# Writing the transposes of the last query tile and of the context's queries later in a hybrid attention kernel

## The chip, the cores and the metric

The kernel runs on one core of one Trainium2 chip. The metric is the device time of one execution in microseconds (us). Before the change it is 1639.22 us, the median of three runs (1639.19 to 1640.38).

## What is computed

Two layers of a trunk are applied to 512 latent tokens and 128 context tokens that share all weights. Each layer is

```
h     = rmsnorm(x) * (1 + scale) + shift
parts = h @ w_in                       # 8 parts
mixed = [ gated linear recurrence | grouped-query attention | differential attention ]
x     = x + gate1 * (mixed @ w_out)
h     = rmsnorm(x) * (1 + scale') + shift'
x     = x + gate2 * (conv_ffn(h))
```

The queries of the grouped attention (8 heads of 64) are normalised per head. Those of the latent tokens are also rotated; those of the context tokens are not. Context tokens attend to context tokens only: 4 groups of 4 score blocks of 128x128 (two groups for the grouped, two for the differential attention). Latent tokens attend to cached context keys and to all latent keys. All is fp32; matrix products split each operand into a rounded part and a rest and add three products.

## The kernel before, in words

The order of the instructions on each engine is written by hand through a small planner. `Flow` keeps a model clock, `fl.now`. Code that emits TensorE products moves the clock on (`fl.step(1296)` after six products, 816 after six narrower ones), and each step first emits the follow-up work whose time has come. `fl.add(delay, fn)` puts work on that list. So a delay does not make the chip wait: it decides behind which products a step is *written*, and each engine then executes its own instructions in the written order. Semaphores, which the tile framework adds, make an instruction wait for its operands and for the buffer it writes.

The part that matters is `mixer`, up to the attention proper. In order:

- Three groups of products (`proj_group`), each four weight chunks by five token tiles by six products of 512 columns: first the queries (`evac_gq` takes the results), then keys, values and differential queries (`evac_kvdq`), then differential keys and values (`evac_dkdv`). The five sums of a group stay in PSUM for the whole group.
- Two narrower sums `lacc` for the recurrence's gate, each in two halves of 24 products of 320 columns; ScalarE reads each half with a Gelu (`lru_in`, L704).
- Then `wait("a")` steps the model clock until 17 pieces of work are written (8 query stacks, 5 key stacks, 4 context groups), and the attention begins with its first scores (L1150).

Between these products TensorE also transposes. For a latent query tile `t` the chain is `s1` (norm), `s2` (rotation), `s2b` (rounded part, GpSimd), `s3` (rest, VectorE, L858), `s4`: four transposes to a tile `qT` (L867) and two ScalarE copies out (L869), once per half of the heads. For the context's queries it is `c2` (VectorE, L878), `c3`: four transposes to `cqT` (L884) and a copy. Key tiles go the same way: `k_stack`, three transposes to `kT` (L905), copies L906 and L910. A key stack needs one of two staging slots ("st"), which query stacks also use.

The context's attention runs beside all this: `ctx_stage` writes four score products (`cS`, L1039), VectorE maxima (`cnm`, L1041) and four ScalarE exponentials (L1044); `ctx_norm` scales the result on VectorE (L1061 to L1068); `ctx_T` transposes it (`cPTp`, L1076) and copies it out (L1078).

PSUM is `pb`: eight single-bank tiles in this part (`psum_mode(0, 8)`). A new tile takes a bank whose last reader has been written, and its first matmul waits until that reader is done. A group's five sums leave three banks for all transposes and context scores; a `cS` of the first two groups takes two of them.

Of the kernel before, what the change touches and what calls it, by code (L numbers as in the profile page):

```python
# [48 lines left out]
GQ = (5150, 3150, 2200, 1400)  # L49


def f32(ap):
    return ap.bitcast(F32)
# [179 lines left out]
def hybrid_kernel(ctx: ExitStack, tc: tile.TileContext, i, o):  # L233
# [13 lines left out]
    fl = Flow()  # L247
    fl.free["st"] = 2

    def half(name, dt=F32):  # L250
        return hpool.tile([128, 2 * W], dt, tag="h", name=name)
# [4 lines left out]
    def tslot(name, n=644, dt=F32):  # L256
        return tp.tile([128, 644], dt, tag="t", name=name)[:, :n]
# [15 lines left out]
    def pb(name, dt=F32):  # L273
        return mode["pb"].tile([128, 512], dt, tag="pb", name=name)
# [5 lines left out]
    def small(name, n=8):  # L280
        return smp.tile([128, 8], F32, tag="sm", name=name)[:, :n]
# [86 lines left out]
    def round_pool(out, in_):  # L368
        pool.tensor_scalar(out=out, in0=in_, scalar1=1.0, scalar2=0.0, op0=ALU.mult, op1=ALU.add)
# [278 lines left out]
    def mixer(l, hh, hl, first=None):  # L648
# [15 lines left out]
        kr, pending = [], {"t": 0.0, "lru": 2, "a": 17}  # L664
# [140 lines left out]
        def rope(src, t, tab, nh, hd):  # L805

            cs, sn = tab[0][:, t], tab[1][:, t]
            e = hd // 4
            tmp = tslot("ropet", nh * hd)
            s5 = src.rearrange("p (h a f e) -> p h a f e", a=2, f=2, e=e)  # L810
            t5 = tmp.rearrange("p (h a f e) -> p h a f e", a=2, f=2, e=e)
            n4 = sn.rearrange("p (a f e) -> p a f e", a=2, f=2)
            for f in range(2):
                dve.tensor_tensor(out=t5[:, :, :, f], in0=s5[:, :, :, 1 - f],
                                  in1=n4[:, :, f].unsqueeze(1).to_broadcast([128, nh, 2, e]), op=ALU.mult)
            s3 = src.rearrange("p (h d) -> p h d", d=hd)
            dve.tensor_tensor(out=s3, in0=s3, in1=cs.unsqueeze(1).to_broadcast([128, nh, hd]), op=ALU.mult)
            dve.tensor_tensor(out=src, in0=src, in1=tmp, op=ALU.add)

        def head_rstd(src, nh):  # L820
            junk = tslot("hsq", nh * 64)
            act.activation(out=junk, in_=src, func=ACTF.Square)
            ss = small("hss", nh)
            dve.tensor_reduce(out=ss, in_=junk.rearrange("p (h d) -> p h d", d=64), op=ALU.add, axis=AX.X)
            return pow_rstd(ss, nh, 1.0 / 64)

        def scale_heads(src, r, nh):
            s3 = src.rearrange("p (h d) -> p h d", d=64)
            dve.tensor_tensor(out=s3, in0=s3, in1=r.unsqueeze(2).to_broadcast([128, nh, 64]), op=ALU.mult)

        def evac_gq(t, a):
            n = tslot("gqr", 512)
            act.activation(out=n, in_=a, func=ACTF.Copy)
            n3 = n.rearrange("p (h d) -> p h d", d=64)
            got = {}

            def s1():
                got["r"] = head_rstd(n, 8)
                if t < 4:
                    fl.add(GQ[1], s2, 2700)  # L840
                else:
                    fl.add(3500, c2, 1300)

            def s2():
                scale_heads(n, got["r"], 8)
                rope(n, t, rope_t["q"], 8, 64)
                for g in range(2):
                    fl.add(100, lambda g=g: s2b(g), 0, "st")

            def s2b(g):  # L850
                st = tslot("gqs", 512, F32R).rearrange("p (h s d) -> p h s d", h=4, s=2)
                hs = slice(4 * g, 4 * g + 4)
                round_pool(st[:, :, g], n3[:, hs])
                fl.add(GQ[2], lambda: s3(g, st), 350)

            def s3(g, st):
                hs = slice(4 * g, 4 * g + 4)
                dve.tensor_tensor(out=st[:, :, 1 - g], in0=n3[:, hs], in1=f32(st[:, :, g]), op=ALU.subtract)  # L858
                fl.add(GQ[3], lambda: s4(g, st))

            def s4(g, st):
                if not qa:
                    for p in range(4):
                        qa[p] = half("qa", F32R)[:, 0:1024].rearrange("p (h c) -> p h c", h=2)
                pt = pb("qT", F32R)
                for h in range(4):
                    pe.transpose(pt[:, h * 128:h * 128 + 128], st[:, h].rearrange("p s d -> p (s d)"), identr)  # L867
                for p in range(2):
                    act.activation(out=qa[2 * g + p][:, :, t * 128:t * 128 + 128],  # L869
                                   in_=f32(pt[:, p * 256:p * 256 + 256].rearrange("p (h c) -> p h c", h=2)),  # L870
                                   func=ACTF.Copy)
                fl.free["st"] += 1
                pending["a"] -= 1
                fl.now += 230

            def c2():
                scale_heads(n, got["r"], 8)
                dve.tensor_tensor(out=n3, in0=n3, in1=rope_t["qg"].unsqueeze(1).to_broadcast([128, 8, 64]), op=ALU.mult)  # L878
                fl.add(2500, c3)

            def c3():
                pt = pb("cqT")
                for b in range(4):
                    pe.transpose(pt[:, b * 128:b * 128 + 128], n[:, b * 128:b * 128 + 128], ident)  # L884
                act.activation(out=cqT, in_=pt[:, 0:512].rearrange("p (b c) -> p b c", b=4), func=ACTF.Copy)
                fl.now += 430

            fl.add(GQ[0], s1, 600)
# [141 lines left out]
        def ctx_probs(qT, kT, kd):  # L1030

            P = tslot("cP", 512).rearrange("p (n c) -> p n c", n=4)
            nm, den, rd = small("cnm", 4), small("cden", 4), small("crd", 4)
# [9 lines left out]
            for n in range(4):  # L1043
                act.activation(out=P[:, n], in_=blkof(n), func=ACTF.Exp, bias=nm[:, n:n + 1], accum_out=den[:, n:n + 1])  # L1044
            return P, den, rd

# [12 lines left out]
        def ctx_norm(n):  # L1059
            P, den, rd = ctxP[n]  # L1060
            dve.reciprocal(out=rd, in_=den)  # L1061
            if n >= 2:
                for j in range(2):
                    dve.tensor_tensor(out=rd[:, 2 * j + 1:2 * j + 2], in0=rd[:, 2 * j + 1:2 * j + 2], in1=neglam[:, l:l + 1],
                                      op=ALU.mult)
            dve.tensor_tensor(out=P, in0=P, in1=rd.unsqueeze(2).to_broadcast([128, 4, 128]), op=ALU.mult)
            if n >= 2:
                dve.tensor_tensor(out=P[:, 0::2], in0=P[:, 0::2], in1=P[:, 1::2], op=ALU.add)  # L1068
            fl.add(CX[3], lambda: ctx_T(n))

        def ctx_T(n):
            P = ctxP[n][0]
            m = 4 if n < 2 else 2
            pt = pb("cPTp")
            for e in range(m):
                pe.transpose(pt[:, e * 128:e * 128 + 128], P[:, e if n < 2 else 2 * e], ident)  # L1076
            dst = cPTg[:, 4 * n:4 * n + 4] if n < 2 else cPTd[n - 2]
            act.activation(out=dst, in_=pt[:, 0:m * 128].rearrange("p (n c) -> p n c", n=m), func=ACTF.Copy)  # L1078
            fl.now += 430
            pending["a"] -= 1  # L1080
# [570 lines left out]
```

## Time and profile before

| | |
|---|---|
| runs | 1639.19, 1639.22, 1640.38 us |
| the profiled execution | 1639.05 us, span 1637.2 us |
| TensorE busy | 1589.8 us, 97% of the span |
| VectorE, ScalarE, GpSimd busy | 58%, 44%, 21% |
| mean granted clock of TensorE | 0.997 of 2.4 GHz |

The profile is of one execution. TensorE works nearly all the time, so an instruction that only moves to another place among its products costs nothing by itself; what matters is where TensorE stands still. A row of the timeline gives the start, the time until the last of the merged instructions ends, and in brackets the idle time just before and what ended it. The modelled end of a matmul lies beyond the start of the next one, so pitches are read from start to start.

### The profile page before, as it was taken

Reading aid. Unit: us, or ns where it says so; the run is one execution under the profiler, and the core shown is the slowest. Engines: PE = TensorE matmul, PEld = TensorE weight load, DVE = VectorE, ACT = ScalarE, POOL = GpSimd, SP = SyncE. Lnnn points to the kernel's source line nnn. Section 1 sums busy time; section 2 is a strip of 40 time slices with the busy share of each in tenths; the row PEclk is TensorE's granted clock in tenths of the full one; section 3 lists DMA queues with packets and bytes.
Section 4 is the critical chain, followed back from the end, with each engine's and each line's share of the span. In section 5 each row is a group of like instructions: output and inputs, shape, how many; then the busy total and the mean of one; then the engine's idle time right before and its main releaser. Section 6 shows DMA issues by size and latency. Waiting matters only on the chain. (4 is left out here: it accounts for less than half of the span.)

```text
span 1637.2 us, 25371 instructions
## 1 busy us (share of the span) xinstructions
PE 1589.8 (97%) x10070; PEld 1396.7 (85%) x10070; DVE 943.5 (58%) x1548; ACT 722.7 (44%) x1476; POOL 351.2 (21%) x782
## 2 busy tenths in 40 slices
PE   6999999999999999999999999999999999999998
PEld 4778776789999889999887787878899998899986
DVE  5687786465555434555467778765555553355544
ACT  4745777544333212333247367774433331133331
POOL 5162443032111000111052614420411100011101
PEclk9999999999999999999999999999999999999999
DMA  9222456412213221222312214352112232121312
GB/s 332 68 87 87 156 192 215 154 52 65 91 52 110 97 77 52 78 78 82 98 33 66 88 60 154 137 187 78 53 52 89 67 129 78 52 78 55 101 65 90
DMA packets 99434, 161.03 MB, mean 98 GB/s; under 512 B 10670, under 2 KB 69222, under 8 KB 94196
## 3 DMA queue, kind: packets, MB, share of 16 engines
q1 hardware_dynamic: 98068, 158.00, 28.9%
q8 instruction: 79, 1.29, 0.3%
q0 software_dynamic: 1040, 1.14, 0.2%
q14 instruction: 39, 0.32, 0.1%
q10 hardware_dynamic: 208, 0.28, 0.0%
HBM read 155.95 MB, written 3.44 MB: 97 GB/s over the span
## 5 line engine op out<-in xcount | busy, mean ns | idle before, releaser
L350 DVE TENSOR_TENSOR wl<-raw,wh 128x1024 fp32r<-128x1024 f32 x180 | 219.9, 1228 | 408.5 <-ACT wh L349 407.5
L365 PE MATMUL uacc<-hl,wh 128*128 128x320 f32 (+2 forms) x1408 | 437.3, 311 | 0.8 <-DVE hl L594 0.5
L364 PE MATMUL uacc<-hh,wh 128*128 128x320 f32 (+2 forms) x1408 | 437.4, 311 | 0.0
L366 PE MATMUL uacc<-hh,wl 128*128 128x320 f32 (+2 forms) x1408 | 435.1, 309 | 0.1
L349 ACT ACTIVATE wh<-raw 128x1024 fp32r<-128x1024 f32 x180 | 189.5, 1058 | 178.9 <-PE tacc L366 156.7
L365 PEld LDWEIGHTS uacc<-hl,wh 128*128 128x128 f32 x1408 | 265.2, 188 | 1.7 <-DVE hl L594 1.6
L366 PEld LDWEIGHTS uacc<-hh,wl 128*128 128x128 f32 x1408 | 265.9, 189 | 0.6 <-DVE wl L350 0.6
L364 PEld LDWEIGHTS uacc<-hh,wh 128*128 128x128 f32 x1408 | 265.5, 189 | 0.3
L364 PE MATMUL tacc<-wh,g 128*128 128x512 f32 x440 | 173.6, 395 | 0.0
L365 PE MATMUL tacc<-wl,g 128*128 128x512 f32 x440 | 173.6, 394 | 0.0
L366 PE MATMUL tacc<-wh,g 128*128 128x512 f32 x440 | 173.1, 393 | 0.0
L1369 POOL TENSOR_SCALAR ca<-u,fcol 128x642 f32<-128x642 f32 x44 | 38.9, 884 | 417.1 <-issue 244.4
L1161 DVE TENSOR_REDUCE nm<-S 128x1 f32<-128x640 f32 x128 | 101.7, 819 | 21.8 <-PE S L1151 11.4
L1176 POOL TENSOR_SCALAR P<-P,den 128x640 f32<-128x640 f32 x96 | 82.5, 865 | 143.4 <-DVE den L1170 77.2
L1165 ACT ACTIVATE P<-S,nm 128x640 f32<-128x640 f32 x128 | 100.8, 792 | 24.9 <-DVE nm L1161 21.4
L1365 ACT ACTIVATE u<-uacc 128x192 f32<-128x192 f32 (+1 forms) x88 | 29.0, 330 | 185.6 <-PE uacc L366 185.6
L366 PEld LDWEIGHTS tacc<-wh,g 128*128 128x128 f32 x440 | 82.7, 188 | 19.4
L364 PEld LDWEIGHTS tacc<-wh,g 128*128 128x128 f32 x440 | 82.6, 188 | 19.3
L365 PEld LDWEIGHTS tacc<-wl,g 128*128 128x128 f32 x440 | 82.7, 188 | 18.9
L364 PE MATMUL acc<-wh,hh 128*128 128x512 f32 x240 | 97.0, 404 | 0.0
L366 PE MATMUL acc<-wh,hl 128*128 128x512 f32 x240 | 95.4, 397 | 0.0
L365 PE MATMUL acc<-wl,hh 128*128 128x512 f32 x240 | 95.2, 397 | 0.0
(292 smaller groups left out, 2667.9 us busy)
## 6 DMA issues: line engine op xcount, KB each, us to landing
raw<-in_ffn_w_up_dram SPq DMA_DIRECT2D x44, 1024.0 KB, 5.1
raw<-in_ada_w_dram SPq DMA_DIRECT2D x40, 1024.0 KB, 4.9
raw<-in_ffn_w_down_dram SPq DMA_DIRECT2D x20, 1024.0 KB, 5.0
raw<-in_w_in_dram SPq DMA_DIRECT2D x16, 1024.0 KB, 8.4
araw<-in_ada_w_dram SPq DMA_DIRECT2D x16, 512.0 KB, 9.5
raw<-in_w_out_dram SPq DMA_DIRECT2D x8, 1024.0 KB, 6.6
gates<-gate SPq DMA_DIRECT2D x8, 512.0 KB
x<-in_x_sample_dram SPq DMA_DIRECT2D x4, 512.0 KB
```

Source lines behind the costliest of these rows:

```text
L349: act.activation(out=wh, in_=raw, func=ACTF.Copy)
L350: dve.tensor_tensor(out=wl, in0=raw, in1=f32(wh), op=ALU.subtract)
L364: pe.matmul(out, lhsT=lh, rhs=rh, start=start, stop=False)
L365: pe.matmul(out, lhsT=lh, rhs=rl, start=False, stop=False)
L366: pe.matmul(out, lhsT=ll, rhs=rh, start=False, stop=stop)
L1161: dve.tensor_reduce(out=box["nm", c], in_=view(c), op=ALU.max, axis=AX.XY, negate=True)
L1165: act.activation(out=box["P"][c].rearrange("p (a b) -> p a b", a=2), in_=view(c), func=ACTF.Exp, bias=box["nm", c], accum_out=box["den"][: ...
L1176: pool.tensor_scalar(out=P[-1], in0=P[-1], scalar1=den[:, 1 + comps:2 + comps], scalar2=0.0, op0=ALU.mult, op1=ALU.add)
L1365: act.activation(out=u[:, 1 + cut:1 + L], in_=acc[1][:, 0:L - cut], func=ACTF.Copy)
L1369: pool.tensor_scalar(out=out, in0=u[:, 1:1 + n], scalar1=wcol(1), scalar2=wcol(3), op0=ALU.mult, op1=ALU.add)
```

## The change

Three edits in `mixer`. The work of `s4` for the last latent query tile (`t == 3`) gets a delay 1500 longer, and `c3` (context queries) one 2000 longer. `ctx_T` puts itself off by 300 as long as more than `4 - n` of the 17 pieces are open, so that the first context transpose is written only after all query and key stacks.

```diff
-                fl.add(GQ[3], lambda: s4(g, st))
+                fl.add(GQ[3] + 1500 * (t == 3), lambda: s4(g, st))
...
-                fl.add(2500, c3)
+                fl.add(4500, c3)
...
         def ctx_T(n):
+            if pending["a"] > 4 - n:
+                return fl.add(300, lambda: ctx_T(n))
```

No instruction is added or removed on any engine; only the order differs, in both layers alike. GpSimd's and SyncE's orders are the same as before. `cqT` moves behind 12 products of the second group. Because the last query stacks free their staging slots later, the key stacks and the context's steps move too.

The first place is TensorE in the third group, where the last query tile (`qT_1364`, `qT_1379` before; `qT_1386`, `qT_1401` now) meets the first context scores (`cS`). Before:

```order
L867 MATMUL qT_1364<-identr_102,gqs_1322 128x128 [waits DVE_49,PE_49,Activation_49]
L867 MATMUL qT_1364<-identr_102,gqs_1322 128x128 x3
L867 MATMUL qT_1379<-identr_102,gqs_1331 128x128 [waits DVE_49,PE_49,Activation_49]
L867 MATMUL qT_1379<-identr_102,gqs_1331 128x128 x3
L1039 MATMUL cS_1398<-cx_581 128x128 [waits PE_49,Activation_49]
L1039 MATMUL cS_1399<-cx_581 128x128 [waits PE_49,Activation_49]
L1039 MATMUL cS_1398<-cx_581 128x128
L1039 MATMUL cS_1399<-cx_581 128x128
```

Now, six products later:

```order
L1039 MATMUL cS_1374<-cx_581 128x128 [waits PE_49,Activation_49]
L1039 MATMUL cS_1375<-cx_581 128x128 [waits PE_49,Activation_49]
L1039 MATMUL cS_1374<-cx_581 128x128
L1039 MATMUL cS_1375<-cx_581 128x128
L867 MATMUL qT_1386<-identr_102,gqs_1322 128x128 [waits DVE_49,PE_49,Activation_49]
L867 MATMUL qT_1386<-identr_102,gqs_1322 128x128 x3
L867 MATMUL qT_1401<-identr_102,gqs_1331 128x128 [waits DVE_49,Activation_49,Pool_49]
L867 MATMUL qT_1401<-identr_102,gqs_1331 128x128 x3
```

The scores now stand directly ahead of the query transposes. In the built program `qT_1401` lies in the bank of `cS_1374`, so it waits for the third of the four exponentials that read those scores.

The second place is 30 products on: the second context scores and the first two key tiles. Before, these two key tiles stood 12 products ahead of the scores. Now:

```order
L1039 MATMUL cS_1470<-cx_581 128x128 [waits DVE_49,Activation_49]
L1039 MATMUL cS_1471<-cx_581 128x128 [waits PE_49,Activation_49]
L1039 MATMUL cS_1470<-cx_581 128x128
L1039 MATMUL cS_1471<-cx_581 128x128
L905 MATMUL kT_1482<-identr_102,gks_1399 128x128 [waits PE_49,Activation_49,Pool_49]
L905 MATMUL kT_1482<-identr_102,gks_1399 128x128
L905 MATMUL kT_1482<-identr_102,gks_1399 128x128 [waits DVE_49]
L905 MATMUL kT_1491<-identr_102,gks_1414 128x128 [waits DVE_49,Activation_49,Pool_49]
L905 MATMUL kT_1491<-identr_102,gks_1414 128x128 x2
```

Here `kT_1491` lies in the bank of `cS_1470` and waits for the exponentials of the second scores.

The third place is ScalarE beside the narrow sums `lacc`, from the third scores' exponentials to the Gelu. Before:

```order
L1044 ACTIVATE cP,cden<-cS,cnm 128x128 x4
L704 ACT_TABLE_LOAD
L704 ACTIVATE lrug<-lacc 128x320
L1044 ACT_TABLE_LOAD
L1044 ACTIVATE cP,cden<-cS,cnm 128x128 x4
L704 ACT_TABLE_LOAD
L704 ACTIVATE lrug<-lacc 128x320
L1078 ACTIVATE cPTg<-cPTp 128x256
```

Now (L1080 is the former L1078):

```order
L1044 ACTIVATE cP,cden<-cS,cnm 128x128 x4
L704 ACT_TABLE_LOAD
L704 ACTIVATE lrug<-lacc 128x320
L906 ACTIVATE kk<-kT 128x2x128
L910 ACTIVATE kl<-kT 64x128 x2
L1080 ACTIVATE cPTg<-cPTp 128x512
L1044 ACT_TABLE_LOAD
L1044 ACTIVATE cP,cden<-cS,cnm 128x128 x4
L1080 ACTIVATE cPTg<-cPTp 128x512
L704 ACT_TABLE_LOAD
L704 ACTIVATE lrug<-lacc 128x320
L1080 ACTIVATE cPTg<-cPTp 128x256
```

Three copies of the last key tile and two of context probabilities stand in this chain now; before, they were written ahead of it. On TensorE the last `cPTp` had nothing of the sums behind it; now six products of `lacc` follow it.

## Rows read from the trace of the kernel before

**Rows 1.** TensorE's waits in layer 1, 105 to 173 us: total, times, longest

```profile
PE qT L867 <- DVE gqs L858: 1.2, 1, 1.2
PE S L1150 <- ACT lrug L704: 0.8, 1, 0.8
PE cqT L884 <- DVE gqr L878: 0.8, 1, 0.8
PE cdkT L1024 <- ACT cdk L1017: 0.5, 1, 0.5
```

**Rows 2.** Timeline of TensorE, layer 1, query transposes: start, us, instruction, [idle before]

```profile
113.58 0.87 PE L867 MATMUL qT<-identr,gqs 128*128 128x128 f32 x8 [1.17 <-DVE gqs L858]
115.25 0.66 PE L884 MATMUL cqT<-ident,gqr 128*128 128x128 f32 x4 [0.79 <-DVE gqr L878]
115.66 0.48 PE L364 MATMUL acc<-wh,hh 128*128 128x512 f32 x1
...
121.30 0.80 PE L867 MATMUL qT<-identr,gqs 128*128 128x128 f32 x8
121.94 0.47 PE L364 MATMUL acc<-wh,hh 128*128 128x512 f32 x1
```

**Rows 3.** Timeline of TensorE, layer 1, context scores and transposes, first attention score

```profile
143.82 0.72 PE L1039 MATMUL cS<-cx 64*128 64x128 f32 x8
144.47 0.66 PE L1076 MATMUL cPTp<-ident,cP 128*128 128x128 f32 x4
...
159.29 0.50 PE L1039 MATMUL cS<-cx 32*128 32x128 f32 x8
...
167.55 0.38 PE L1076 MATMUL cPTp<-ident,cP 128*128 128x128 f32 x2
...
171.33 0.38 PE L1076 MATMUL cPTp<-ident,cP 128*128 128x128 f32 x2
172.51 0.41 PE L1150 MATMUL S<-kk,qa 128*128 128x320 f32 x1 [0.80 <-ACT lrug L704]
```

**Rows 4.** Timeline of VectorE, layer 1: maxima of the first two scores, gate product

```profile
134.62 0.76 DVE L1041 TENSOR_REDUCE cnm<-cS 128x2 f32<-128x256 f32 x2 [0.44 <-PE cS L1039]
...
144.57 0.76 DVE L1041 TENSOR_REDUCE cnm<-cS 128x2 f32<-128x256 f32 x2 [0.83 <-PE cS L1039]
...
168.78 0.83 DVE L709 TENSOR_TENSOR lrug<-lrug,lruS 128x640 f32<-128x640 f32 x1 [3.28 <-ACT lrug L704]
```

**Rows 5.** Timeline of ScalarE, layer 1: exponentials, copies of probabilities and keys

```profile
135.14 1.28 ACT L1044 ACT_TABLE_LOAD   x1 [0.56 <-DVE cnm L1041]
136.44 0.37 ACT L1044 ACTIVATE cP<-cS,cnm 128x128 f32<-128x128 f32 x1
...
137.14 0.36 ACT L1044 ACTIVATE cP<-cS,cnm 128x128 f32<-128x128 f32 x1
...
145.79 0.37 ACT L1044 ACTIVATE cP<-cS,cnm 128x128 f32<-128x128 f32 x1
...
146.73 0.60 ACT L1078 ACTIVATE cPTg<-cPTp 128x512 f32<-128x512 f32 x1
147.23 0.38 ACT L906 ACTIVATE kk<-kT 128x256 fp32r<-128x256 f32 x1
...
148.05 0.39 ACT L906 ACTIVATE kk<-kT 128x256 fp32r<-128x256 f32 x1
```

**Rows 6.** ScalarE's busy time from the third exponentials to the gate's Gelu

```profile
core 0: us, ACT busy (x), PEclk, DMA share, GB/s
162.40:168.80 6.40, 6.31 (x15) 1.00 0.18 73
```

**Rows 7.** Busy time by stretch: length, PE, PEld, DVE, ACT, POOL, granted clock, DMA

```profile
111.90:115.60 3.70, 1.74 (x14) 1.16 (x13) 3.63 (x7) 2.32 (x9) 0.59 (x1) 1.00 0.87 310
...
915.70:919.40 3.70, 1.67 (x14) 1.12 (x13) 3.63 (x7) 2.32 (x9) 0.55 (x1) 1.00 0.90 321
919.90:923.30 3.40, 3.40 (x10) 2.66 (x9) 0.99 (x5) 1.31 (x5) 2.54 (x6) 0.51 0.00 0
```

## The prediction

> **What bounds the kernel now.** I read the page first: TensorE is busy 97% of the span and the chain that ended last runs over it, so only its standstills and its clock can move the time. The list of TensorE's waits between the second group of products and the first attention score is next [rows 1]. It shows that this stretch holds four waits of 3.3 us together, in each of the two layers. The wait for `cqT` (0.8) is the one that the change aims at; the wait for the first `qT` (1.2) stays, since that transpose isn't moved. The timeline of TensorE shows the two waits as one hole: eight transposes between a wait of 1.17 and one of 0.79, and then the products go on at 115.66 [rows 2]. The busy time by stretch shows a second cost of the same hole: in the second layer TensorE was busy 1.67 of 3.70 us there, and right behind it the granted clock is 0.51 for 3.40 us, the lower of the two levels, 1.2 GHz. The twin hole of the first layer (1.74 of 3.70) left the next clock at 1.00 [rows 7]. So such a hole may or may not cost a fall of the clock.
>
> The last query tile, which the change also moves, has no wait in that list. Nothing can be won there directly.
>
> **The change, part by part.** All sums are for one layer; both layers have the same order.
>
> *A, the moved `cqT`.* In an undisturbed place eight transposes start at 121.30, end at 122.10, and the next product starts at 121.94, 0.16 before that end [rows 2]. Here the eight end at 113.58 + 0.87 = 114.45, so with `cqT` gone the products can start at 114.29, not 115.66: 1.37 us earlier. The four transposes themselves take 115.25 to 115.66, 0.41, at their new place, where VectorE has long delivered: A = -0.96. The ScalarE copy behind them moves along; its reader (the first scores) stands more than 50 products later.
>
> *B, query transposes behind the first scores.* PSUM has eight banks, five are held by the group's sums. The scores take two of the other three, the first four query transposes the third, and the next four have only a bank of the scores. They wait for VectorE's maxima, ScalarE's table load and three exponentials, and every product behind them waits too, as TensorE takes its matmuls in order. The price comes from the same chain before, when nothing waited for it. From a score's start T to the maxima 144.57 - 143.82 = 0.75 [rows 3, 4]; from the maxima at 134.62 to the end of the third exponential at 137.14 + 0.36 = 137.50, with the load of 1.28 in it, 2.88 [rows 4, 5]. So the bank is free at T + 3.63. TensorE gets there at T + 0.65 (143.82 to 144.47) [rows 3] plus four transposes, half of 0.64 [rows 2]: T + 0.97. B = +2.66. VectorE can't be late here: it has nothing else written ahead of these maxima. Before, the order was the other way round (the scores waited for a query tile's copy), which was cheap since a copy is short.
>
> *C, key transposes behind the second scores.* The same count of banks: the first key tile takes the third bank, the second waits for the exponentials. No table load this time: the third exponential ends at 145.79 + 0.37 = 146.16, 2.34 after the scores' start at 143.82 [rows 3, 5]. TensorE gets there after 0.65 and three transposes of 0.08: 0.89. C = +1.45. If VectorE is late with these maxima it is more.
>
> *D.* Two context transposes (`cPTp`, 0.41 each like `cqT`) that stood ahead of the third scores now stand behind them, where D = -0.82 is gained for the moment. The key tile that filled a part of the wait for `cdkT` (0.5) [rows 1] leaves too, but that wait ends on a ScalarE copy at the same distance from the last product, so I cost it at nothing.
>
> So the third scores start -0.96 + 2.66 + 1.45 - 0.82 = 2.33 later than before.
>
> *E, from the third scores to the attention.* Before, this took 159.29 to 172.51 [rows 3], and ScalarE sets it: from 162.40 to 168.80 it is busy 6.31 of 6.40 us [rows 6] with table loads, exponentials and Gelus; VectorE's gate product waits 3.28 for that Gelu [rows 4], the last normalisation queues behind it on VectorE, and the last `cPTp` at 171.33 behind that. The change writes five copies into this chain: twice `cPTg` (146.73 to 147.23, 0.50 each) and three of a key tile (147.23 to 148.05, 0.82) [rows 5]: +1.82. Six products now follow the last `cPTp`; 24 of them and two transposes took 167.55 to 171.33 [rows 3], so six are 0.9, of which the last copy hides some: I take +0.6. VectorE now stands idle while it waits for the first scores and does that work later, so the third maxima may be late. No row prices this: the bounds are 0 and 1.3, half of B; near the lower end, as VectorE regains time during C, I take 0.3. E = +2.7, between 1.8 and 4.0.
>
> *F, the clock.* The old fall goes: the hole shrinks to one wait. Running 3.40 us at 0.51 cost 0.49 x 3.40 = 1.67 [rows 7]. But B makes a hole with a single wait of 2.66, more than the two old waits together (1.96) [rows 2]. Since one of two holes of the old size was followed by a fall, I take one fall behind each B and none behind C: -1.67 + 2 x 1.67 = +1.67.
>
> GpSimd's and SyncE's written orders are unchanged. The weight splits move by a few rows on ScalarE and VectorE, but each is written a whole chunk of 30 products before its use.
>
> **The sum.** Two layers of 2.33 + 2.7 = 5.03 are 10.1, with the clock 11.7. The profiled execution is 1639.05 us, 0.17 under the median of the runs. Forecast: 1639.05 + 11.7 = 1650.8 us, slower by 0.7%. About 0.2% (3.3 us) can be told from no change.
>
> **A page against a row.** The load in B took 1.28 and the exponential started at 136.44, 0.02 behind its end [rows 5]. The Trainium skill (ScalarE: Activation LUTs, section "What ACT_TABLE_LOAD costs") gives 1283 ns for the load and 1380 ns for a drain with it, 2.66 us per switch. By that page B would be 1.38 larger and the sum 2.8 us higher; the trace shows the load and no drain.
>
> **The rivals.**
> - *Faster: the banks are free in time.* The mechanism is B's chain with another result: if the exponentials of the first scores ended by T + 0.97, B and C would be nothing, no copies would be late, and A and the old fall would stand alone: 1639.05 - 1.92 - 1.67 = 1635.5. For it: no wait for a bank of over 0.5 stands in the list [rows 1]. Against it: the chain holds a load of 1.28 and needs 3.63. It decides at 2.66 us of slack that I don't find. Chance 0.05.
> - *About the same.* B and C shrink to under half, and E's copies fit into gaps: within 3.3 us of before. Chance 0.05.
> - *E is hidden.* The copies run while ScalarE would wait anyway, so only the 2.33 remain: 1639.05 + 4.7 + 1.67 = 1645.4. Against it: 6.31 of 6.40 busy [rows 6]. Chance 0.12.
> - *No new fall of the clock.* 1639.05 + 10.1 - 1.67 = 1647.5. For it: the twin hole in the first layer [rows 7]. Chance 0.20.
> - *A fall behind every B and every C.* 1639.05 + 10.1 + 3 x 1.67 = 1654.2. Chance 0.14.
> - *Each load drains as well.* If a time as long as the load's own row, 1.28, followed the load in B, two layers would give 2.6 more: 1653.4. Against it stand the 0.02 above. Chance 0.02. This is the page's rule worked out from a row.
>
> **How the numbers follow.** The forecast keeps 0.42. The range reaches from just under the case with E hidden to the case with four falls and VectorE late by a further half microsecond or so per layer: 1645.0 to 1655.5. It leaves out the first two rivals, and the outer ends of the others. Slower by over 0.2% are all cases but the first two: 0.90. Faster 0.05, within 0.2% 0.05.
>
> **What would show it.** In the profile after the change: no wait of `cqT`; a wait of `qT` for ScalarE's `cP` (L1044) of about 2.7 us, once per layer; one of `kT` for `cP` of about 1.4; the first attention score about 5 us later after its group's start; the granted clock at the lower level behind the first of these waits, and not behind the hole at the second group. It is wrong if the list of TensorE's waits has no row of `qT` on `cP`, if that row stays under 1 us, or if the stretch from the third scores to the first attention score is no longer than before.

## The result and the profile after

| | before | changed | ratio, 95% interval |
|---|---|---|---|
| first comparison, 5 runs each | 1639.19 us | 1652.11 us (1646.80 to 1654.77) | 1.0073 [1.0062, 1.0084] |
| second comparison, 11 and 6 runs | 1638.98 us | 1650.80 us (1647.54 to 1653.94) | 1.0079 [1.0065, 1.0093] |

The change makes the kernel 12 to 13 us slower, 0.7 to 0.8%. The profiled execution of the first comparison took 1646.80 us (span 1645.0), the shortest of its five. Its TensorE is as busy as before, 97%:

```profile
PE 1588.9 (97%) x10070; PEld 1394.8 (85%) x10070; DVE 944.5 (57%) x1548; ACT 722.5 (44%) x1476; POOL 349.9 (21%) x782
```

The list of TensorE's waits in layer 1, 105 to 180 us, answers to [rows 1] (total, times, longest; from L1072 on a line number is 2 higher than before):

```profile
PE qT L867 <- ACT cP L1044: 2.6, 1, 2.6
PE kT L905 <- DVE kr L817: 1.4, 1, 1.4
PE qT L867 <- DVE gqs L858: 1.3, 1, 1.3
PE cPTp L1078 <- DVE cP L1068: 0.9, 1, 0.9
PE cdkT L1024 <- ACT cdk L1017: 0.7, 1, 0.7
PE kT L905 <- DVE gks L898: 0.6, 1, 0.6
PE S L1152 <- ACT lrug L704: 0.5, 1, 0.5
PE cPTp L1078 <- ACT lrug L704: 0.4, 1, 0.4
```

Four waits of 3.3 us together [rows 1] have become eight of 8.4. The wait of `cqT` is gone, as intended. The timeline of TensorE shows where the new ones stand; it answers to [rows 2, 3]:

```profile
113.76 0.88 PE L867 MATMUL qT<-identr,gqs 128*128 128x128 f32 x8 [1.25 <-DVE gqs L858]
117.34 0.60 PE L884 MATMUL cqT<-ident,gqr 128*128 128x128 f32 x4
...
133.70 0.72 PE L1039 MATMUL cS<-cx 64*128 64x128 f32 x8
134.35 0.53 PE L867 MATMUL qT<-identr,gqs 128*128 128x128 f32 x4
...
137.50 0.50 PE L867 MATMUL qT<-identr,gqs 128*128 128x128 f32 x4 [2.62 <-ACT cP L1044]
...
146.51 0.72 PE L1039 MATMUL cS<-cx 64*128 64x128 f32 x8
147.15 0.45 PE L905 MATMUL kT<-identr,gks 128*128 128x128 f32 x3
...
149.03 0.43 PE L905 MATMUL kT<-identr,gks 128*128 128x128 f32 x3 [1.42 <-DVE kr L817]
...
163.08 0.50 PE L1039 MATMUL cS<-cx 32*128 32x128 f32 x8
...
177.65 0.41 PE L1078 MATMUL cPTp<-ident,cP 128*128 128x128 f32 x2 [0.93 <-DVE cP L1068]
179.46 0.42 PE L1152 MATMUL S<-kk,qa 128*128 128x320 f32 x1 [0.53 <-ACT lrug L704]
```

Both halves of step B and of step C are there: four query transposes behind the first scores go, the other four stand 2.62 us; three key transposes behind the second scores go, the next three stand 1.42 us. The list names VectorE's `kr` for that second wait. `kr` isn't an input of these transposes (they read `gks`); the experiments below show that the exponentials end it. Layer 2 has the same waits to 0.1 us.

ScalarE's timeline shows what the first wait is made of (start, us, then the instruction):

```profile
134.95 1.28 ACT L1044 ACT_TABLE_LOAD   x1 [6.15 <-DVE cnm L1041]
136.24 0.37 ACT L1044 ACTIVATE cP<-cS,cnm 128x128 f32<-128x128 f32 x1
...
136.94 0.36 ACT L1044 ACTIVATE cP<-cS,cnm 128x128 f32<-128x128 f32 x1
```

The third exponential ends at 136.94 + 0.36 = 137.30, 3.60 behind the scores' start at 133.70; the transposes start at 137.50.

Where the time went, by stretches between instructions of TensorE (us; one star for each time that the lower clock, 1.2 GHz, was granted in the stretch). The second profile is of the changed kernel too, from the last experiment below:

| stretch | before | changed | changed, second profile |
|---|---|---|---|
| layer 1: second group's first `qT` to first attention score | 58.93 | 65.70* | 64.14 |
| to the first product behind the attention (`tacc`, L364) | 128.87 | 127.39 | 128.72 |
| to layer 2's first `qT` of the second group | 615.97* | 614.88 | 617.41** |
| to layer 2's first attention score | 60.53* | 64.08 | 65.70* |
| to `tacc` | 121.79 | 121.53 | 121.83 |

Without the lower clock the first row grows by 64.14 - 58.93 = 5.21, and the fourth by 64.08 - (60.53 - 1.67) = 5.22. The whole loss lies in these two stretches.

### The profile page after: what moved, and what is told of

Its sections match the earlier page's. It is cut to its first block, busy times and chain, and to the rows that moved or that the text cites. A ratio compares the mean times of both kernels' runs of the same rounds, so it can differ in the third digit from the quotient of the medians.

```text
span 1645.0 us, 25370 instructions
## 1 busy us (share of the span) xinstructions
PE 1588.9 (97%) x10070; PEld 1394.8 (85%) x10070; DVE 944.5 (57%) x1548; ACT 722.5 (44%) x1476; POOL 349.9 (21%) x782
## 5 line engine op out<-in xcount | busy, mean ns | idle before, releaser
L364 PE MATMUL uacc<-hh,wh 128*128 128x320 f32 (+2 forms) x1408 | 437.4, 311 | 0.0
L364 PEld LDWEIGHTS uacc<-hh,wh 128*128 128x128 f32 x1408 | 265.5, 189 | 0.3
L364 PE MATMUL tacc<-wh,g 128*128 128x512 f32 x440 | 173.6, 395 | 0.0
L364 PEld LDWEIGHTS tacc<-wh,g 128*128 128x128 f32 x440 | 82.6, 188 | 19.3
L364 PE MATMUL acc<-wh,hh 128*128 128x512 f32 x240 | 96.9, 404 | 0.0
```

What stands on the lines that cost most here:

```text
L364: pe.matmul(out, lhsT=lh, rhs=rh, start=start, stop=False)
```

## The experiments

Each ratio is to the kernel before, whose runs stood on the same chip (medians 1638.05 to 1639.14).

### The change without its first edit

```diff
-                fl.add(GQ[3] + 1500 * (t == 3), lambda: s4(g, st))
+                fl.add(GQ[3], lambda: s4(g, st))
```

> The change without its first edit: the last query tile stays where it was before, ahead of the first context scores; the moved cqT and the held-back context transposes stay. My theory (banks): steps B and C, and with them the copies of step E, come from the first edit alone. So there is no wait of qT or kT for cP, A gives 2 x 0.96, the old fall of the clock (1.67) goes, and the time is about 1635.5 us, up to 1638 if the held-back transposes cost something at the end of the narrow sums. Rival 1 (the held-back context transposes and their copies before the attention cost most): the waits go but the attention still starts late, about 1644 us. Rival 2 (the moved cqT starts the delay): as slow as the changed kernel, about 1650 us.

1635.16 us, 0.9976 [0.9967, 0.9984]: faster than before. The list of TensorE's waits in layer 1:

```profile
PE qT L867 <- DVE gqs L858: 1.2, 1, 1.2
PE S L1152 <- ACT lrug L704: 0.8, 1, 0.8
PE cdkT L1024 <- ACT cdk L1017: 0.7, 1, 0.7
PE S L1152 <- ACT P L1167: 0.7, 1, 0.7
```

No wait on the context's probabilities is left. The first edit alone costs about 15.6 us (1650.8 to 1635.2). Both rivals fall.

### The moved `cqT` alone, and everything but it

The first kernel is before with `fl.add(4500, c3)` only; the second is the changed kernel with `fl.add(2500, c3)`.

> The kernel before with the moved cqT alone, no other edit. My theory: the hole at the second group loses its second wait, 0.96 us in each of two layers, 1637.3 us, and 1635.6 if the fall of the clock behind that hole in the second layer goes with it. Rival 1 (the wait only moves to another place): the sum of TensorE's waits stays and the time is 1639.2. Rival 2 (the moved cqT takes a bank or pushes work behind it): slower than before by 1 us or more.

1635.49 us, 0.9981 [0.9972, 0.9990]. The held-back context transposes, the only difference to the run above, cost and win nothing that can be told. From the second group's hole to the first scores, layer 2 takes 19.11 us (914.47 to 933.58) against 21.60 before (917.35 to 938.95), of which 1.67 is the clock: A is -0.82. (Layer 1, where no clock fell: 19.18 against 20.02, -0.84.)

> The change with cqT back at its old place. My theory: the two holes at the second group have both waits again, so this is slower than the changed kernel by 1.9 us (about 1654 us), and by 1.67 more if a fall of the clock returns there; the waits of qT and kT for cP stay at 2.6 and 1.4 per layer. Rival (the moved cqT takes part in the delay): at or below the changed kernel's 1652 us.

1654.56 us, 1.0089 [1.0069, 1.0109]. That is 3.8 above the changed kernel's 1650.8, but of four runs, and the two intervals overlap; the profile is the firmer evidence. The waits for `cP` stay at 2.62 and 1.4. The hole has its second wait again (0.79): from it to the first scores layer 1 takes 20.86 us against 19.94 in the changed kernel, and in layer 2 the lower clock follows it.

### Later scores instead of an earlier tile

```diff
-CX = (3000, 4000, 4000, 3000, 6000, 12000, 8000)
+CX = (3000, 4000, 4000, 3000, 6000, 15000, 8000)
```

> The changed kernel with the context's score steps written later by 3000 on the planner's clock, so that the late query tile stands ahead of the first scores again and the first two key tiles ahead of the second. All three edits of the change stay. My theory (the order of scores and transposes costs, not the lateness of the tile): the waits of qT and kT for cP are under 0.5 us, and the time is near that of the kernel without the first edit (1635.2), 1635 to 1639 us. Rival (the tile itself, or the held-back context transposes, come too late for the attention): the waits for cP go, but others of the same size come before the attention, and the time stays above 1645.

1635.59 us, 0.9984 [0.9975, 0.9994]. The timeline of TensorE shows the old order at the new, later place, and no wait in brackets:

```profile
133.51 0.80 PE L867 MATMUL qT<-identr,gqs 128*128 128x128 f32 x8
...
137.08 0.71 PE L1039 MATMUL cS<-cx 64*128 64x128 f32 x8
...
142.01 0.62 PE L905 MATMUL kT<-identr,gks 128*128 128x128 f32 x6
```

The tile is as late as the change makes it, and all three edits stand. So the lateness of the tile costs nothing that can be told from the kernel without the first edit; its place behind the scores does.

### What the wait is for: table load and bank

To the changed kernel this adds an exponential that loads the table ahead of the scores:

```diff
+            if n == 0:
+                act.activation(out=small("pre", 1), in_=epsc, func=ACTF.Exp)
```

> The changed kernel and one added operation: an exponential of one column on ScalarE, written just ahead of the first context scores, so that the table is loaded before the maxima come. It computes nothing that is used. My theory: the wait of qT for cP (2.62) holds the table load of 1.28, so it shrinks to about 1.34 in each layer, the wait of kT stays at 1.4, and the time falls by 2.6 us, by up to 1.67 more for each fall of the clock that goes with the shorter hole: 1645 to 1649.5 us. Rival 1 (the wait is for VectorE's maxima or for the bank's other readers, and the load lies beside it): the wait stays at 2.6 and the time at 1652. Rival 2 (the load also drains ScalarE): the wait shrinks by more than 1.6.

1645.77 us, 1.0041 [1.0027, 1.0055], 5.0 less than the changed kernel. Timeline of TensorE, layer 1:

```profile
135.94 0.51 PE L867 MATMUL qT<-identr,gqs 128*128 128x128 f32 x4 [1.34 <-DVE kr L817]
```

The wait falls from 2.62 to 1.34, by exactly the 1.28 of the load's row, while the wait of `kT` stays at 1.43. In layer 2 it falls to 1.62 only: there the first exponential starts 1.54 behind the scores instead of 1.27, just as the second of VectorE's two maxima ends; why it does so there alone stays open. So the load is in series with the wait, and nothing of its size comes with it. The waits account for 2.3 of the 5.0 us; the rest can't be split between falls of the clock and the spread of four runs.

The next one changes only the order of the exponentials that read the scores' two banks:

```diff
-            for n in range(4):
+            for n in (0, 2, 1, 3):
```

> The changed kernel with the four exponentials of a context score step in the order 0, 2, 1, 3: the two that read the bank which the late query tile takes come first and second, not first and third. My theory (the wait is for that bank): the wait of qT for cP falls by one exponential, 0.35, from 2.62 to 2.27, and that of kT from 1.42 to 1.07, in both layers; with the same falls of the clock 1.4 us less, about 1650.7. Rival (the wait is for ScalarE's work as a whole, for VectorE, or for another bank): both waits stay as they are.

1648.98 us, 1.0069 [1.0055, 1.0082]. Timeline of TensorE, layer 1:

```profile
138.96 0.50 PE L867 MATMUL qT<-identr,gqs 128*128 128x128 f32 x4 [2.27 <-ACT cP L1044]
...
150.12 0.42 PE L905 MATMUL kT<-identr,gks 128*128 128x128 f32 x3 [1.08 <-DVE ropet L814]
```

Both waits lose one exponential, 0.35 and 0.34, as the bank theory has it. (The medians differ by 1.8 us, but their intervals overlap; the waits are the evidence.) The same amount of ScalarE's work is done at the same time; only which bank comes free first is another. This also settles the wait that the list puts down to VectorE.

### The chain before the attention

VectorE's gate product behind the last normalisation, in the changed kernel:

```diff
-                fl.add(800, mul, 700)
+                fl.add(3500, mul, 700)
```

> The changed kernel with VectorE's gate product (L709) written 2700 later, behind the last normalisation of the context's probabilities instead of ahead of it. TensorE's order is the same. My theory (step E is a chain: ScalarE's Gelu ends late, the gate product waits for it, the normalisation queues behind it, the last cPTp waits for that): the wait of the last cPTp (0.93) goes in both layers, 1.9 us, and the time is about 1650 against 1652. Rival 1 (the last cPTp waits for the exponentials themselves, which ScalarE does late): the wait stays within 0.3. Rival 2 (the gate product then delays the maxima of the attention's first scores): the wait goes and comes back as a wait of S, and the time stays.

1646.32 us, 1.0051 [1.0035, 1.0068]. VectorE in layer 1, first the changed kernel, then this one:

```profile
175.14 0.83 DVE L709 TENSOR_TENSOR lrug<-lrug,lruS 128x640 f32<-128x640 f32 x1 [4.37 <-ACT lrug L704]
...
177.08 0.43 DVE L1068 TENSOR_TENSOR cP<-cP 128x256 f32<-128x256 f32 x1
```

```profile
172.64 0.42 DVE L1068 TENSOR_TENSOR cP<-cP 128x256 f32<-128x256 f32 x1
173.67 0.82 DVE L709 TENSOR_TENSOR lrug<-lrug,lruS 128x640 f32<-128x640 f32 x1 [0.61 <-ACT lrug L704]
```

The normalisation now ends ahead of the gate product, and the last `cPTp` finds its data. Its wait of 0.93 is gone in both layers: this link of E is real. The gain is larger than the 1.9 expected: from the third scores to the first attention score it takes 15.23 and 15.27 us in the two layers instead of 16.38 and 16.37, 2.25 less, and the attention's second scores lose their wait of 0.65 in layer 1 as well. By the medians it is 4.5, of four runs here.

The same edit in the change without its first edit and in the kernel before, where the last `cPTp` has no wait:

> The change without its first edit, and the gate product written 2700 later as in the run with the changed kernel. Here the last cPTp has no wait, so my theory is that this edit has nothing of step E to win: 0 to 0.65 us per layer, by the wait of the second attention scores for ScalarE's probabilities, 1634.0 to 1635.2 us against 1635.16. Rival (the gate product is late work for the attention in any order): 2 to 4 us faster, 1631 to 1633.

> The kernel before with the gate product 2700 later and nothing else. My theory: the last cPTp had no wait before the change, so this changes at most 1.3 us: 1637 to 1639. Rival (the gate product costs in any order): 2 to 4 us faster.

1636.49 us, 0.9990 [0.9981, 0.9999], and 1638.49 us, 0.9998 [0.9989, 1.0007]. Nothing is won, and the first is even 1.3 us above what it was without the edit; in its layer 2 a wait of the attention for ScalarE's probabilities grows from 0.44 to 0.87. So the gate product's place only matters where the first edit has made the chain late.

### The first query tile later

The change without its first edit, and this:

```diff
-                fl.add(GQ[3], lambda: s4(g, st))
+                fl.add(GQ[3] + 1300 * (t == 0), lambda: s4(g, st))
```

> The change without its first edit, and the FIRST query tile's transposes later by 1300, which takes them from the hole at the second group. My theory: the wait of 1.2 for gqs goes too in each layer; if nothing else moves, 2.4 us and the falls of the clock behind that hole, so 1632.5 us against 1635.2. Rival (the tile meets later steps, whose banks and copies then come later): small waits of 0.4 to 0.9 appear at the context's scores and transposes instead, and the time is 1634 to 1637, no better than without this edit.

1634.49 us, 0.9979 [0.9970, 0.9987], the lowest median of the study, but 0.7 from the kernel without the first edit, whose ratio is even a little lower (0.9976): the two can't be told apart. Timeline of TensorE, layer 1:

```profile
113.60 0.82 PE L867 MATMUL qT<-identr,gqs 128*128 128x128 f32 x8
...
124.67 0.30 PE L1002 MATMUL ckT<-ident,kd 128*128 128x128 f32 x1 [0.71 <-DVE kd L993]
```

The wait of 1.25 goes, and 0.71 at `ckT` and 0.25 at the second scores come: the rival's picture. With the gate product later in addition:

> The kernel with the first query tile later (1634.49) and the gate product 2700 later. By my theory 0 to 1.3 us faster than that kernel, 1633.2 to 1634.5; this is the candidate for the fastest version. Rival as above: 1630.5 to 1632.5.

1636.09 us, 0.9986 [0.9977, 0.9995]: no gain on top.

### The changed kernel once more

> The changed kernel once more, since its profiled execution (1646.80 us) was the shortest of five and their median 5.3 us longer. My theory: executions of this kernel differ only by how many falls of the clock they take, 1.67 us each; so TensorE's waits at the second query, the context scores and the attention are the same to 0.1 us, and the profiled time stands above or below 1646.8 by about 1.7 for each fall more or less than the one found there. The median of more runs is 1649 to 1653 us. Rival (the waits themselves vary, by the arrival of DMA data): the wait of qT for cP or the waits before the attention differ by more than 0.3 between the two profiles.

1650.80 us; the profiled execution took 1650.84. Up to the attention all waits are the same to 0.1 us, in both layers. Three rows of TensorE's timeline in layer 1, first query tile of the second group, third scores, first attention score:

```profile
113.63 0.87 PE L867 MATMUL qT<-identr,gqs 128*128 128x128 f32 x8 [1.23 <-DVE gqs L858]
...
161.37 0.50 PE L1039 MATMUL cS<-cx 32*128 32x128 f32 x8
...
177.77 0.41 PE L1152 MATMUL S<-kk,qa 128*128 128x320 f32 x1 [0.53 <-ACT lrug L704]
```

The clock isn't the same. Busy time by stretch (columns as in [rows 7]), behind the wait of 2.62 in layer 1 and in layer 2, of the first profile and of this one:

```profile
138.30:141.70 3.40, 3.40 (x11) 2.58 (x10) 2.85 (x6) 1.49 (x3) 0.77 (x2) 0.53 0.00 0
945.90:949.30 3.40, 3.40 (x16) 2.74 (x16) 2.85 (x7) 1.76 (x4) 1.05 (x2) 1.00 0.02 5
```

```profile
138.10:141.50 3.40, 3.40 (x17) 2.74 (x16) 2.81 (x7) 1.56 (x4) 0.83 (x2) 1.00 0.00 0
948.40:951.80 3.40, 3.40 (x10) 2.71 (x9) 2.84 (x6) 1.45 (x3) 0.72 (x2) 0.55 0.02 5
306.30:313.10 6.80, 6.33 (x14) 4.70 (x15) 2.31 (x3) 2.51 (x3) 0.00 (x0) 0.50 0.46 167
```

The first has its fall of the clock in layer 1, the second in layer 2, and the second has a long one behind the attention too. So the rival falls where it was put, before the attention. Elsewhere waits do vary: at the end of layer 1's attention, those for the conditioning weights. TensorE's waits there, before, in the first profile of the changed kernel, and in this one:

```profile
PE adaT L526 <- DVE arow L516: 1.7, 1, 1.7
PE ada L507 <- DMA raw<-in_ada_w_dram: 1.6, 2, 0.9
```

```profile
PE adaT L526 <- DVE arow L516: 1.2, 1, 1.2
...
PE ada L507 <- DMA raw<-in_ada_w_dram: 0.5, 1, 0.5
```

```profile
PE adaT L526 <- DVE arow L516: 1.5, 1, 1.5
PE ada L507 <- DMA raw<-in_ada_w_dram: 1.4, 2, 0.7
```

That is 3.3, 1.7 and 2.9 us.

## Why the prediction was right, step by step

The forecast (slower, 1650.8 us) held, and so did its mechanism: the moved transposes take the scores' banks and TensorE stands behind them. That the second comparison's median is 1650.80 to the hundredth is luck: six runs spread from 1647.5 to 1653.9, the first comparison gave 1652.11, and below two errors of the sum go against each other. The terms, without the clock:

| term, per layer | predicted | measured |
|---|---|---|
| A, moved `cqT` | -0.96 | -0.82 |
| B, wait of `qT` | +2.66 | 2.62 |
| C, wait of `kT` | +1.45 | 1.42 |
| first four steps (A to D): third scores later | +2.33 | second profile 161.37 - 113.63 = 47.74, before 159.29 - 113.58 = 45.71 [rows 2, 3]: +2.03 |
| E, third scores to attention | +2.7 (1.8 to 4.0) | 179.46 - 163.08 = 16.38, before 172.51 - 159.29 = 13.22: +3.16 |
| sum | +5.03 | 5.21 and 5.22 |

**B and C** were read from a chain on which nothing waited before, and came within 0.04. The runs with the early table and with the other order of the exponentials show both links, the load of 1.28 and the bank.

**D** was taken at -0.82. The measured A, B and C leave 2.03 - 3.22 = -1.19 for it. By the written order that is the last key tile, which I costed at nothing: it now stands behind the third scores as well; a wait of `cdkT` that is 0.22 longer (0.75, before 0.53) is already in that number.

**E** was a chain on ScalarE, and its rows give the terms one by one. First exponential of the third scores and the Gelu before the gate product, before and changed:

```profile
160.93 0.37 ACT L1044 ACTIVATE cP<-cS,cnm 128x128 f32<-128x128 f32 x1 [3.50 <-DVE cnm L1041]
...
168.31 0.44 ACT L704 ACTIVATE lrug<-lacc 128x320 f32<-128x320 f32 x1
```

```profile
165.47 0.37 ACT L1044 ACTIVATE cP<-cS,cnm 128x128 f32<-128x128 f32 x1 [4.47 <-DVE cnm L1041]
...
174.67 0.44 ACT L704 ACTIVATE lrug<-lacc 128x320 f32<-128x320 f32 x1
```

| part of E, layer 1 | predicted | measured |
|---|---|---|
| third scores to first exponential (maxima late) | +0.3 | 2.39, before 1.64: +0.75 |
| to the Gelu (five copies) | +1.82 | 9.20, before 7.38: +1.82 |
| Gelu to first attention score (six products) | +0.6 | 4.79, before 4.20: +0.59 |

In layer 2 the three are +0.95, +1.82 and +0.41. So the copies came out as read from the rows; the part that was mis-sized is the late maxima, the one that no row priced. In the changed kernel this chain runs on into the gate product and the normalisation without a gap of over 0.15 us, up to the last `cPTp` at 177.65. It isn't the only long path, though. With the gate product taken out of it the stretch is still 15.23, 2.0 more than before. Seen from TensorE, the changed kernel's 3.16 are waits of 0.56, 0.44, 0.93 and 0.53 in place of one of 0.80, together 1.66 more, and 1.50 that is not standing. By the written order most of the 1.50 is the work that the change moves behind the third scores, the two `cPTp` of step D among it: their 0.82 was gained for the moment and is paid again here. The gate product's link is shown by its run; that the copies alone cause the rest is read from rows, not shown by a run without them.

**F, the clock,** is the step that was not right. I took one fall for the old holes and one behind every B. Over all profiles of this study in which the hole at the second group has both waits (before, the run with `cqT` back, the run of before with the gate product), 3 of 6 such holes were followed by the lower clock. Where only the wait for `gqs` is left, none of 18 was. So the first half is right: without the second wait the fall goes. Behind B (waits of 2.27 to 2.62) it came in 7 of 10, behind B of 1.3 to 1.6 in 1 of 2, behind C in none of 12. That makes about one old fall against 1.4 new ones per execution, not one against two: +0.6 us instead of +1.67. The counts are small. A fall behind B does cost about what was taken: 65.70 - 64.14 = 1.56 in layer 1, 65.70 - 64.08 = 1.62 in layer 2. Once, in layer 1 of the run with `cqT` back, it lasted twice as long: the granted clock was 0.50 from 137.5 to 143.9 us. Put together, the two layers' stretches add 10.4 where 10.1 was forecast, and the clock adds 0.6 where 1.67 was: 1639.05 + 10.4 + 0.6 = 1650.1.

The profiled 1646.80 then comes out as 1639.05 + 5.2 + 5.2 (both layers) - 1.67 (old fall) + 1.6 (one new one) = 1649.4, less 1.1 (615.97 to 614.88: the fall behind layer 1's attention, at 302 us before, did not come in that execution) and less 1.5 (128.87 to 127.39: mainly the shorter waits at its end). Neither of these belongs to the change: the second profile has them back.

**The page.** The Trainium skill (ScalarE: Activation LUTs, section "What ACT_TABLE_LOAD costs") gives 2.66 us for a switch, load and drain. Taking the switch out of the wait took out 1.28, not 2.66, and the exponential starts 0.01 behind the load's end (134.95 + 1.28 = 136.23, next row 136.24). In this chain the measurement decides for the load alone.

The rivals on the clock forecast times that single executions reach: 1647.5 without a new fall (1646.80, 1647.54, 1648.02 were measured), 1654.2 with a fall behind every B and C (1653.63 to 1654.77). The times alone don't bear them out. The execution of 1646.80 had a fall behind B in layer 1 and was short for the other reasons just given; the long ones were not profiled, and no profile has a fall behind C.

## What to carry to other kernels

Before a transposing or evacuating step is written later, count the banks that are free at its new place and name the instruction that frees the next one: behind a score product that is not a short copy but a softmax's maxima, table load and exponentials, and an in-order TensorE stops all its products for it. The price can be read before the change is made, from the chain that runs there while nothing waits for it. Where several small delays are changed at once, try each alone: here one of three (the moved `cqT`) brings all of the 3.6 us gain and another loses 15.6.

## What the runs showed of the hardware

- The same hole in the same program is followed by the lower clock in one execution and not in the next (layer 1 in one profile of the changed kernel, layer 2 in the other). Its 11 runs spread over 8 us (1646.80 to 1654.77), and their mean granted clocks go from 0.999 in the short ones to 0.991 in the longest.
- What a fall costs depends on where it lies. From `tacc` to layer 2's hole, profiles without a fall took 614.6 to 614.9 us (the changed kernel, the moved `cqT` alone, the other order of the exponentials, the first query tile and the gate product later). With one just behind `tacc` and no other, three took 616.0 to 616.1 (the kernel before, the run with `cqT` back, the early table), 1.1 to 1.5 more where the clock alone lost 1.7. With one near 840 us and no other, the changed kernel with the gate product later took 614.96, 0.1 to 0.4 more. With a long one behind the attention and another near 845 us the second profile took 617.4, 2.5 to 2.8 more, although the long one alone lost 0.50 x 6.80 = 3.4 us of clock.
- The waits around the conditioning weights at the end of layer 1's attention were 1.7 us in one execution of the changed kernel and 2.9 in another, and 3.3 in one of the kernel before, with nothing changed near them.
